# The state-space branch's state and output matmuls, each as four column tiles of 32

## The chip, the core and the metric

The kernel runs on one core of a Trainium2 chip. The metric is the device time of one execution, in microseconds (us). The engines are TensorE (PE; its weight loads are listed apart as PEld), VectorE (DVE), ScalarE (ACT), GpSimd (POOL) and SyncE (SP), which issues all transfers of this kernel. Each engine works through a queue of its own, in order, and waits at an instruction whose operands are not ready.

## What is computed

The program is a trunk of two layers on 256 tokens of width 1024. Each layer is a SwiGLU block, then four mixers side by side (RG-LRU, latent attention, sparse attention with an indexer, and S5), merged under gates, then a second SwiGLU block; every block is modulated by a vector that a product with `ada_w` gives. The change is in the S5 mixer. Cut to what matters here:

```python
def s5_branch(u, lam_re, lam_im, log_dt, b_re, b_im, c_re, c_im, d, w_glu, b_glu):
    # 32 groups of 16 channels, 64 complex states in each group
    ...
    ug = u.reshape(bsz, t, S5_GROUPS, S5_GROUP)
    bu_re = jnp.einsum('gpj,btgj->btgp', bb_re, ug)
    bu_im = jnp.einsum('gpj,btgj->btgp', bb_im, ug)
    _, _, x_re, x_im = lax.associative_scan(complex_combine, (a_re, a_im, bu_re, bu_im), axis=1)
    y = (jnp.einsum('gjp,btgp->btgj', c_re, x_re)
         - jnp.einsum('gjp,btgp->btgj', c_im, x_im))
    y = y.reshape(bsz, t, D_S5) + d * u
    y = jax.nn.gelu(y)
    return y * jax.nn.sigmoid(y @ w_glu + b_glu)
```

## The kernel before

**S5 by chunks.** The 256 tokens are 64 chunks of 4. Two groups of 16 channels make a pair, and there are 16 pairs `q`; one pair's 2 x 16 channels times 4 tokens of a chunk are the 128 partitions of `vv`, its 2 x 64 states the 128 rows of a state tile, and the 64 chunks are the moving columns. So every S5 matmul has 128 partitions, 128 stationary columns and 64 moving columns, in fp32. `s5_states` has four steps `h` in a layer; each puts 8 matmuls (2 parts z, real and imaginary, by 4 pairs) into one PSUM bank (L863), and DVE then turns, scans and turns back that bank and writes `F`, the state at the start of each chunk. `s5_out_prep` makes the stationary tiles for the outputs: `wo` (state to output) and `tz` (input of the chunk to its output); its own products, L817 and L820, are already written as four tiles of 32 columns (`tile_position=(0, 32 * qq)`), each tile with another moving operand. `s5_out` has two halves `h` of 8 pairs each; for each pair it adds up three products in PSUM, `tz` by `vv` (L898) and twice `wo` by `F` (L900). ACT and DVE make the GELU of each half.

**The precise products.** The large weights are fp32 and come by DMA into `raw` tiles. ACT rounds a tile to `hi` (the cast L237), DVE subtracts to get `lo` (through the helper at L103), and a product is three matmuls in the rounded type: `mm3` at L244 to L246, with weights moving, and `mm3w` at L249 to L251, with weights stationary. DVE operations go through helpers, so that L103, L106 and L109 are lines of helpers (tensor by tensor, scalar by tensor by tensor, tensor by scalar), L118 and L116 are copies on DVE and ACT, L112 is ACT's activation. `ada` (L277) also works in four tiles of 32 columns.

**What sets the order.** One string, `ORDER`, lists the stages of the mixers (S1 are the four steps of `s5_states`, S2 those of `s5_out_prep` and `s5_out`, m the steps of latent attention, g and p and t products for gates and merge). From the program in that order a scheduler sets each engine's queue. SBUF tiles are taken by tag from pools of a fixed number of buffers, and a tile waits until an earlier one of its tag is released: tag `s5p` has 7, and `tz`, `wo`, the merge's sums (`s5p_merge`) and the queries of latent attention (`s5p_mla`) all have it; `hi` and `lo` have 4 each, PSUM's `acc` has 4 and `up` 2.

**Latent attention beside it.** Around the outputs' run stands the first half of the heads: the product with `w_uq`, ACT's copy of it (L1306), the sums of squares (L1309), the scale `msc_mla` (L109, L1311), the rope of q (DVE, `s_rope` and `s5p_mla`), the transposes of q on PE (L1321), then the product with `w_ukv`, and the transposes of k (L1349). The matmuls of gate products (`ps_up_gate`) and of `tok_gemm` fill PE between them.

Of the kernel before, what the change touches and what calls it, by code (L numbers as in the profile page):

```python
# [78 lines left out]
def tile_trunk(ctx, tc, a, out, probe=None):  # L79
    nc = tc.nc  # L80
    V, S, T, G = nc.vector, nc.scalar, nc.tensor, nc.gpsimd
# [11 lines left out]
    def bank(tag, shape=(128, 512)):  # L93
        uid[0] += 1
        return ps.tile(list(shape), F32, tag="ps_" + tag, name=f"ps_{tag}_{lbl()}_{uid[0]}",
                       bufs=dict(acc=4, up=2, tp=1, ms=1)[tag])
# [17 lines left out]
    def cp(o, x, on_act):  # L114
        if on_act:
            S.copy(o, x)  # L116
        else:
            V.tensor_copy(o, x)  # L118
# [121 lines left out]
    def wpiece(w, k0, k, c0, n):  # L240
        return w[k0 * 128:(k0 + k) * 128, c0:c0 + n].rearrange("(k p) c -> p k c", p=128)
# [537 lines left out]
    def s5_out_prep(st):  # L779
# [49 lines left out]
        st["S2"] = (wo, tz)  # L829
        yield  # L830

    def w_stationary(w, c0, uh, ul, evac):

        for m in range(4):
            wt = W(8, 128, [(slice(0, 128), wpiece(w, 0, 8, c0 + 128 * m, 128))])
            p = bank("acc")
            for k in range(KD):
                mm3w(p[:, 0:256], wt.hi[:, k], wt.lo[:, k], uh[:, k], ul[:, k], k == 0, k == KD - 1)
            evac(m, p[:, 0:256])
# [6 lines left out]
    def s5_states(us, st):  # L846
        vv = new("b4", (128, 16, 64))
        v5 = vv.rearrange("p (b q) c -> p b q c", q=4)
        for i in range(4):
            for qq in range(4):  # L850
                o = v5[32 * i:32 * i + 32, :, qq, :]
                x = us[32 * qq:32 * qq + 32].rearrange("p b (c i) -> p b c i", i=4)[:, :, :, i]
                cp(o, x, KN["v"][qq])
        yield
        F = []
        st["S1"] = (vv, F)
        for h in range(4):
            qs = slice(4 * h, 4 * h + 4)
            p = bank("acc", (128, 2, 4, 64))
            for z in range(2):  # L860
                for q in range(4):
                    qg = 4 * h + q
                    T.matmul(p[:, z, q, :], st["wi"][z][qg // 8][:, qg % 8, :], vv[:, qg, :], start=True, stop=True)  # L863

            t = [new("p2", (128, 2, 4, 64)) for _ in range(2)]
            cs, sn = (bc(st[x][:, None, qs, :], (128, 2, 4, 64)) for x in ("cs", "sn"))
            tt(t[0], p, cs, OP.mult)
            tt(t[1], p, sn, OP.mult)
            tt(t[0][:, 0], t[0][:, 0], t[1][:, 1], OP.add)
            tt(t[0][:, 1], t[0][:, 1], t[1][:, 0], OP.subtract)  # L870
            fl = lambda x: x.rearrange("p q c -> p (q c)")
            mg = fl(st["mg"][:, qs])
            for z in range(2):
                V.tensor_tensor_scan(fl(t[1][:, z]), mg, fl(t[0][:, z]), 0.0, OP.mult, OP.add)

            if h % 2 == 0:
                zz = new("b4", (128, 2, 2, 4, 64))
            z = zz[:, h % 2]
            V.memset(z[:, :, :, 0:1], 0.0)
            d = slice(0, 63)  # L880
            tt(t[0], t[1], cs, OP.mult)
            tt(t[1], t[1], sn, OP.mult)
            tt(z[:, 0, :, 1:64], t[0][:, 0, :, d], t[1][:, 1, :, d], OP.subtract)
            tt(z[:, 1, :, 1:64], t[1][:, 0, :, d], t[0][:, 1, :, d], OP.add)
            F.append(z)
            yield

    def s5_out(l, st, r):
        yield from s5_out_prep(st)
        vv, F = st["S1"]  # L890
        wo, tz = st["S2"]
        y2 = new("b4", (128, 16, 64))
        for h in range(2):
            p = bank("acc", (128, 8, 64))
            for q in range(8):
                qg = 8 * h + q
                z = F[qg // 4]
                T.matmul(p[:, q, :], tz[h][:, q, :], vv[:, qg, :], start=True, stop=False)  # L898
                for zz in range(2):
                    T.matmul(p[:, q, :], wo[zz][h][:, q].rearrange("p i j -> p (i j)"), z[:, zz, qg % 4, :],  # L900
                             start=False, stop=(zz == 1))
            w = new("p2", (128, 8, 64))
            act(w, p, AF.Square)
            ts(w, w, 0.044715 * GK, GK, OP.mult, OP.add)
            tt(w, w, p, OP.mult)
            act(w, w, AF.Tanh)
            stt(y2[:, 8 * h:8 * h + 8], w, 1.0, p, OP.add, OP.mult)
            if h == 0:
                yield
        yc = new("b4", (128, 4, 256))  # L910
        y5 = y2.rearrange("p (b q) c -> p b q c", q=4)
        for i in range(4):
            for qq in range(4):
                o = yc[32 * qq:32 * qq + 32].rearrange("p b (c i) -> p b c i", i=4)[:, :, :, i]
                x = y5[32 * i:32 * i + 32, :, qq, :]
                cp(o, x, KN["y"][qq])
        show(f"s5y{l}", yc)
        r["yc"] = yc
        yield
# [675 lines left out]
    st = {}  # L1595
# [64 lines left out]
```

## Time and profile before

| | |
|---|---|
| time, median of 3 runs | 1500.77 us (1494.9 to 1513.13) |
| the profiled execution's own time | 1495.38 us |
| its span, first to last instruction | 1493.6 us |
| granted TensorE clock, mean of the span | 0.99 of full speed |
| PE / DVE / ACT busy | 1413.4 / 1175.4 / 770.0 us |
| DMA, mean over the span | 210 GB/s |

The profile is one execution; its times are counted from the span's start. Busy time is the union of an engine's instructions, including the time that a matmul is under way in the array, so neighbouring matmuls overlap and the distance from one start to the next says more than the length of one. Every fp32 matmul of the code has two records under PE (and two loads under PEld), every matmul in the rounded type has one. The two layers have the same code and the same order within the mixers; the first layer's S1 and S2 lie between 309 and 409 us, the second's from 1036 us on.

### The profile page before, as it was taken

How to read it: one execution, taken by the hardware profiler on the slowest of the kernel's cores; microseconds unless marked ns; L12 is line 12 of the kernel's file. 1: busy time of each engine (PE TensorE's matmuls, PEld its weight loads, DVE VectorE, ACT ScalarE, POOL GpSimd, SP SyncE). 2: the span in 40 equal slices, each digit the busy share in tenths (PEclk: the TensorE clock that was granted, in tenths of full speed). 3: DMA queues.
4: the chain of work that ended last, by engine and by line, in shares of the span. 5: the costliest groups of instructions: out<-in, count | busy, mean ns of one | idle time of the engine just before them, and what ended most of it. 6: DMA issues, size and time to landing. Idle time of an engine off the chain costs nothing.

```text
span 1493.6 us, 26644 instructions
## 1 busy us (share of the span) xinstructions
PE 1413.4 (95%) x10310; PEld 1262.7 (85%) x10310; DVE 1175.4 (79%) x2027; ACT 770.0 (52%) x1223; POOL 64.0 (4%) x75
## 2 busy tenths in 40 slices
PE   8899999899998998999989998999999999999998
PEld 4588987789888897999968887879988879799997
DVE  4598988789897577988787888777998956866655
ACT  4444456654475645544453445568445655544442
POOL 0000000001011000000010000000100100000000
PEclk9999999999999999999999999999999999999999
DMA  9788888786435365899977878755653535567762
GB/s 287 236 288 291 280 260 258 228 222 174 114 117 138 99 187 181 286 328 317 320 252 250 271 254 276 246 135 143 174 146 95 140 94 164 162 214 227 235 203 99
DMA packets 242087, 313.24 MB, mean 210 GB/s; under 512 B 28088, under 2 KB 169256, under 8 KB 241960
## 3 DMA queue, kind: packets, MB, share of 16 engines
q1 hardware_dynamic: 241960, 311.53, 67.0%
q8 instruction: 81, 1.33, 0.4%
q14 instruction: 46, 0.38, 0.1%
HBM read 310.41 MB, written 1.07 MB: 209 GB/s over the span
## 4 chain that ended last, share of the span: by engine, by line
PE 55%; DVE 21%; DMA 11%; issue 6%; ACT 5%; POOL 1%; SPq 1%; POOLq 0%; DVEq 0%; ACTq 0%
DVE lo_genexpr L103 7%; DMA raw_ada<-in_ada_w_dram 5%; PE ps_up_up_half L249 5%; PE ps_up_up_half L250 5%; PE ps_up_up_half L251 5%; DMA raw_init<-in_ffn_w_dram 4%; PE ps_acc_down_proj L246 3%; PE ps_acc_down_proj L245 3%; PE ps_acc_down_proj L244 3%; PE ps_up_gate L250 3%; ACT hi_genexpr L237 3%; PE ps_up_gate L249 3%; PE ps_up_gate L251 3%; DVE acc_ada L106 2%; PE ps_up_merge L250 2%
## 5 line engine op out<-in xcount | busy, mean ns | idle before, releaser
L237 ACT CAST hi_genexpr<-raw_init 128x1024 fp32r<-128x1024 f32 (+2 forms) x430 | 441.1, 1028 | 497.2 <-PE ps_up_up_half L250 127.4
L103 DVE TENSOR_TENSOR lo_genexpr<-raw_init,hi_genexpr 128x1024 fp32r<-128x1024 f32 (+2 forms) x430 | 511.5, 1193 | 152.5 <-ACT hi_genexpr L237 150.1
L249 PE MATMUL ps_up_up_half<-uh_new_u,hi_genexpr 128*128 128x256 f32 x1216 | 339.2, 279 | 4.2 <-DVE p_silu_cols L106 1.6
L250 PE MATMUL ps_up_up_half<-ul_new_u,hi_genexpr 128*128 128x256 f32 x1216 | 337.4, 278 | 0.0
L251 PE MATMUL ps_up_up_half<-uh_new_u,lo_genexpr 128*128 128x256 f32 x1216 | 337.2, 278 | 0.1
L249 PEld LDWEIGHTS ps_up_up_half<-uh_new_u,hi_genexpr 128*128 128x128 f32 x1216 | 228.8, 188 | 9.8 <-issue 7.5
L250 PEld LDWEIGHTS ps_up_up_half<-ul_new_u,hi_genexpr 128*128 128x128 f32 x1216 | 228.7, 188 | 1.4
L251 PEld LDWEIGHTS ps_up_up_half<-uh_new_u,lo_genexpr 128*128 128x128 f32 x1216 | 228.2, 188 | 0.7 <-DVE lo_genexpr L103 0.7
L106 DVE SCALAR_TENSOR_TENSOR acc_ada<-raw_ada,c_col_tile_trunk,acc_ada 128x1024 f32<-128x1024 f32 x105 | 134.4, 1280 | 28.6 <-DMA raw_ada<-in_ada_w_dram 28.2
L250 PE MATMUL ps_up_gate<-ul_new_u,hi_genexpr 128*128 128x256 f32 x512 | 144.8, 283 | 0.0
L249 PE MATMUL ps_up_gate<-uh_new_u,hi_genexpr 128*128 128x256 f32 x512 | 144.6, 282 | 0.0
L251 PE MATMUL ps_up_gate<-uh_new_u,lo_genexpr 128*128 128x256 f32 x512 | 143.6, 280 | 0.0
L246 PE MATMUL ps_acc_down_proj<-hi_genexpr,yT_mul_cols 128*128 128x512 f32 x288 | 114.6, 398 | 0.0
L244 PE MATMUL ps_acc_down_proj<-hi_genexpr,yT_mul_cols 128*128 128x512 f32 x288 | 114.5, 397 | 0.0
L245 PE MATMUL ps_acc_down_proj<-lo_genexpr,yT_mul_cols 128*128 128x512 f32 x288 | 114.3, 397 | 0.1
L249 PEld LDWEIGHTS ps_up_gate<-uh_new_u,hi_genexpr 128*128 128x128 f32 x512 | 96.4, 188 | 3.0 <-issue 2.2
L251 PEld LDWEIGHTS ps_up_gate<-uh_new_u,lo_genexpr 128*128 128x128 f32 x512 | 96.7, 189 | 0.9 <-issue 0.8
L250 PEld LDWEIGHTS ps_up_gate<-ul_new_u,hi_genexpr 128*128 128x128 f32 x512 | 96.4, 188 | 1.1 <-issue 1.0
L244 PEld LDWEIGHTS ps_acc_down_proj<-hi_genexpr,yT_mul_cols 128*128 128x128 f32 x288 | 54.1, 188 | 13.1 <-issue 1.6
L245 PEld LDWEIGHTS ps_acc_down_proj<-lo_genexpr,yT_mul_cols 128*128 128x128 f32 x288 | 54.2, 188 | 12.6 <-DVE lo_genexpr L103 0.6
L246 PEld LDWEIGHTS ps_acc_down_proj<-hi_genexpr,yT_mul_cols 128*128 128x128 f32 x288 | 54.1, 188 | 12.3
L244 PE MATMUL ps_up_tok_gemm<-hi_genexpr,uh_new_u 128*128 128x424 f32 (+2 forms) x88 | 33.8, 385 | 2.7 <-ACT gt_gate L112 2.7
(474 smaller groups left out, 2698.1 us busy)
## 6 DMA issues: line engine op xcount, KB each, us to landing
raw_init<-in_ffn_w_dram SPq DMA_DIRECT2D x240, 512.0 KB
raw_ada<-in_ada_w_dram SPq DMA_DIRECT2D x128, 512.0 KB
raw_init<-in_w_in_dram SPq DMA_DIRECT2D x96, 512.0 KB
raw_init<-in_w_branch_dram SPq DMA_DIRECT2D x24, 512.0 KB
raw_init<-in_ffn_w_dram SPq DMA_DIRECT2D x36, 256.0 KB
raw_init<-in_w_out_dram SPq DMA_DIRECT2D x16, 512.0 KB
s5p_load<-in_ada_w_dram SPq DMA_DIRECT2D x16, 256.0 KB
s5p_load<-in_ada_w_dram SPq DMA_DIRECT2D x8, 512.0 KB
```

The costliest lines, as they stand in the source:

```text
L103: eng.tensor_tensor(o, x, y, op)
L106: V.scalar_tensor_tensor(o, x, s, y, op0, op1)
L237: S.copy(self.hi, self.raw)
L244: T.matmul(o, xh, wh, start=first, stop=False)
L245: T.matmul(o, xh, wl, start=False, stop=False)
L246: T.matmul(o, xl, wh, start=False, stop=last)
L249: T.matmul(o, wh, xh, start=first, stop=False)
L250: T.matmul(o, wh, xl, start=False, stop=False)
L251: T.matmul(o, wl, xh, start=False, stop=last)
```

## The change

A helper `col_tiles` issues one old matmul as four: tile `j` has stationary columns 32j to 32j+31, the whole moving operand, and writes partitions 32j to 32j+31 of the same place in PSUM. The three calls of S5 (states, and both kinds of output products) go through it, and the four tiles follow one another by turns. All lines behind the helper move down by 6: L863, L898 and L900 become L836, L1321 becomes L1327. The 160 matmuls of both layers become 640.

```diff
@@ -829,6 +829,12 @@
         st["S2"] = (wo, tz)
         yield
 
+    def col_tiles(o, wt, x, start, stop):
+
+        for j in range(4):
+            c = slice(32 * j, 32 * j + 32)
+            T.matmul(o[c], wt[:, c], x, start=start, stop=stop, tile_position=(0, 32 * j))
+
     def w_stationary(w, c0, uh, ul, evac):
 
         for m in range(4):
@@ -860,7 +866,7 @@
             for z in range(2):
                 for q in range(4):
                     qg = 4 * h + q
-                    T.matmul(p[:, z, q, :], st["wi"][z][qg // 8][:, qg % 8, :], vv[:, qg, :], start=True, stop=True)
+                    col_tiles(p[:, z, q, :], st["wi"][z][qg // 8][:, qg % 8, :], vv[:, qg, :], True, True)
 
             t = [new("p2", (128, 2, 4, 64)) for _ in range(2)]
             cs, sn = (bc(st[x][:, None, qs, :], (128, 2, 4, 64)) for x in ("cs", "sn"))
@@ -895,10 +901,10 @@
             for q in range(8):
                 qg = 8 * h + q
                 z = F[qg // 4]
-                T.matmul(p[:, q, :], tz[h][:, q, :], vv[:, qg, :], start=True, stop=False)
+                col_tiles(p[:, q, :], tz[h][:, q, :], vv[:, qg, :], True, False)
                 for zz in range(2):
-                    T.matmul(p[:, q, :], wo[zz][h][:, q].rearrange("p i j -> p (i j)"), z[:, zz, qg % 4, :],
-                             start=False, stop=(zz == 1))
+                    col_tiles(p[:, q, :], wo[zz][h][:, q].rearrange("p i j -> p (i j)"), z[:, zz, qg % 4, :],
+                              False, zz == 1)
             w = new("p2", (128, 8, 64))
             act(w, p, AF.Square)
             ts(w, w, 0.044715 * GK, GK, OP.mult, OP.add)
```

On PE, at the first states step of the first layer, the order before is this (a name is tag, function, and two numbers; `ps_acc_s5_states` is the bank that the step fills, x4 says that four alike follow one another):

```order
L250 MATMUL ps_up_gate_623_3323<-ul_new_u_480_2577,hi_genexpr_629_3362 128x256
L251 MATMUL ps_up_gate_623_3323<-uh_new_u_479_2576,lo_genexpr_630_3363 128x256
L863 MATMUL ps_acc_s5_states_632_3397<-b4_s5_states_607_3211,s5p_s5_prep_280_1401 128x64 x4
L863 MATMUL ps_acc_s5_states_632_3397<-b4_s5_states_607_3211,s5p_s5_prep_282_1403 128x64 x4
L277 MATMUL ps_ms_ada_621_3291<-raw_ada_641_3428,c_col_tile_trunk_10_86 32x256 x4
L249 MATMUL ps_acc_w_stationary_642_3434<-uh_new_u_479_2576,hi_genexpr_639_3424 128x256
```

and now:

```order
L250 MATMUL ps_up_gate_623_3323<-ul_new_u_480_2577,hi_genexpr_629_3362 128x256
L251 MATMUL ps_up_gate_623_3323<-uh_new_u_479_2576,lo_genexpr_630_3363 128x256
L836 MATMUL ps_acc_s5_states_632_3397<-b4_s5_states_607_3211,s5p_s5_prep_280_1401 32x64 x16
L836 MATMUL ps_acc_s5_states_632_3397<-b4_s5_states_607_3211,s5p_s5_prep_282_1403 32x64 x16
L277 MATMUL ps_ms_ada_621_3291<-raw_ada_641_3452,c_col_tile_trunk_10_86 32x256 x4
L249 MATMUL ps_acc_w_stationary_642_3458<-uh_new_u_479_2576,hi_genexpr_639_3448 128x256
```

Each run of four matmuls of 128 columns has become sixteen of 32, in the same place, and what stands ahead and behind (a gate product, and ada's tiled one) is as it was.

On PE, at the first transposes of q of latent attention (L1321, now L1327), behind the outputs' run of the first layer and the product with `w_ukv`, before (`ps_up_gate_862` is the gate product between them, `hi_genexpr` and `lo_genexpr` its split weights, `s5p_mla_815` the queries):

```order
L250 MATMUL ps_up_gate_862_4749<-ul_new_u_480_2577,hi_genexpr_864_4752 128x256
L251 MATMUL ps_up_gate_862_4749<-uh_new_u_479_2576,lo_genexpr_865_4753 128x256
L249 MATMUL ps_up_gate_862_4749<-uh_new_u_479_2576,hi_genexpr_867_4782 128x256
...
L249 MATMUL ps_up_gate_862_4749<-uh_new_u_479_2576,hi_genexpr_867_4782 128x256
L1321 MATMUL ps_tp_mla_830_4576<-cst_tile_trunk_4_75,s5p_mla_815_4531 96x128 x4
L250 MATMUL ps_up_gate_862_4749<-ul_new_u_480_2577,hi_genexpr_867_4782 128x256
```

and now:

```order
L836 MATMUL ps_acc_s5_out_835_4788<-b4_s5_states_693_3819,s5p_s5_out_prep_730_4037 32x64 x4
L244 MATMUL ps_acc_mla_844_4917<-hi_genexpr_841_4912,mlh_mla_in_525_2756 128x512
...
L246 MATMUL ps_acc_mla_846_4926<-hi_genexpr_841_4912,mll_mla_in_526_2757 128x512
L249 MATMUL ps_up_gate_862_4989<-uh_new_u_479_2576,hi_genexpr_864_4992 128x256
L1327 MATMUL ps_tp_mla_830_4672<-cst_tile_trunk_4_75,s5p_mla_815_4627 96x128 x4
L250 MATMUL ps_up_gate_862_4989<-ul_new_u_480_2577,hi_genexpr_864_4992 128x256
L251 MATMUL ps_up_gate_862_4989<-uh_new_u_479_2576,lo_genexpr_865_4993 128x256
```

Ahead of the transposes stood 34 matmuls of the gate product, 24 with one weight tile and 10 with the next; now there is 1, and the other 33 are behind.

On DVE, at the rope of the same queries, before:

```order
L109 TENSOR_SCALAR msc_mla_817_4533<-mqs_mla_816_4532 128x8
L103 TENSOR_TENSOR lo_genexpr_875_4845<-raw_init_873_4842,hi_genexpr_874_4844 128x1024
L1311 TENSOR_SCALAR msc_mla_817_4533<-msc_mla_817_4533 128x8
L103 TENSOR_TENSOR s1_rope_825_4565<-s5p_mla_815_4531,tm_attn_prep_472_2541 128x128
...
L109 TENSOR_SCALAR p2_s5_out_834_4614<-p2_s5_out_834_4614 128x512
L103 TENSOR_TENSOR s5p_mla_815_4531<-s1_rope_825_4565,s1_rope_826_4566 128x8x16
L103 TENSOR_TENSOR s5p_mla_815_4531<-s1_rope_827_4567,s1_rope_828_4568 128x8x16
L103 TENSOR_TENSOR p2_s5_out_834_4614<-p2_s5_out_834_4614,ps_acc_s5_out_833_4589 128x512
L103 TENSOR_TENSOR lo_genexpr_880_4878<-raw_init_878_4875,hi_genexpr_879_4877 128x1024
L118 COPY s5p_mla_829_4575<-ps_tp_mla_830_4576 96x512
```

and now:

```order
L109 TENSOR_SCALAR msc_mla_817_4629<-mqs_mla_816_4628 128x8
L103 TENSOR_TENSOR s1_rope_825_4661<-s5p_mla_815_4627,tm_attn_prep_472_2541 128x128
L103 TENSOR_TENSOR s1_rope_826_4662<-s5p_mla_815_4627,tm_attn_prep_472_2541 128x128
L1317 TENSOR_SCALAR msc_mla_817_4629<-msc_mla_817_4629 128x8
...
L109 TENSOR_SCALAR p2_s5_out_834_4782<-p2_s5_out_834_4782 128x512
L103 TENSOR_TENSOR s5p_mla_815_4627<-s1_rope_825_4661,s1_rope_826_4662 128x8x16
L103 TENSOR_TENSOR s5p_mla_815_4627<-s1_rope_827_4663,s1_rope_828_4664 128x8x16
L103 TENSOR_TENSOR p2_s5_out_834_4782<-p2_s5_out_834_4782,ps_acc_s5_out_833_4685 128x512
L109 TENSOR_SCALAR p2_s5_out_836_4885<-p2_s5_out_836_4885 128x512
L118 COPY s5p_mla_829_4671<-ps_tp_mla_830_4672 96x512
L103 TENSOR_TENSOR lo_genexpr_875_5085<-raw_init_873_5082,hi_genexpr_874_5084 128x1024
```

The split `lo_genexpr_875` stood ahead of the rope (`s1_rope`) and now stands behind the copy of the transposed queries, 11 rows later; the rope's own rows keep their order. The same holds for the second layer. Further on, the transposes of k (L1349, now L1355) had 22 matmuls of `tok_gemm` between them and what stands ahead, and now have 5. The orders of SP and POOL are the same row for row.

## Rows read from the trace of the kernel before

**Rows 1.** The page's first part: busy us, share of span, instructions.

```profile
PE 1413.4 (95%) x10310; PEld 1262.7 (85%) x10310; DVE 1175.4 (79%) x2027; ACT 770.0 (52%) x1223; POOL 64.0 (4%) x75
```

**Rows 2.** The page's fourth part, the chain that ended last, by engine.

```profile
PE 55%; DVE 21%; DMA 11%; issue 6%; ACT 5%; POOL 1%; SPq 1%; POOLq 0%; DVEq 0%; ACTq 0%
```

**Rows 3.** Groups of instructions: tiles, shapes, count, busy us, mean ns, idle ahead.

```profile
L900 PE MATMUL ps_acc_s_out<-b_s_states,s5p_s_out_prep 128*128 128x64 f32 x128 | 19.5, 275 | 0.0
...
L863 PE MATMUL ps_acc_s_states<-b_s_states,s5p_s_prep 128*128 128x64 f32 x128 | 15.2, 272 | 0.9 <-DVE r_gate L106 0.9
...
L898 PE MATMUL ps_acc_s_out<-b_s_states,s5p_s_out_prep 128*128 128x64 f32 x64 | 12.3, 273 | 0.0
```

**Rows 4.** Timeline of PE, 394 to 412: start us, length us, instruction.

```profile
398.31 0.33 PE L898 MATMUL ps_acc_s_out<-b_s_states,s5p_s_out_prep 128*128 128x64 f32 x2
...
408.95 0.48 PE L244 MATMUL ps_acc_mla<-hi_genexpr,mlh_mla_in 128*128 128x512 f32 x1
...
410.41 0.28 PE L249 MATMUL ps_up_gate<-uh_new_u,hi_genexpr 128*128 128x256 f32 x1
410.53 0.28 PE L250 MATMUL ps_up_gate<-ul_new_u,hi_genexpr 128*128 128x256 f32 x1
```

**Rows 5.** Timeline of PE, 337.4 to 339.9, a states burst.

```profile
337.64 1.89 PE L863 MATMUL ps_acc_s_states<-b_s_states,s5p_s_prep 128*128 128x64 f32 x16
339.34 0.36 PE L249 MATMUL ps_up_gate<-uh_new_u,hi_genexpr 128*128 128x256 f32 x1
```

**Rows 6.** Timeline of PE, 380.3 to 383, tiled products of out_prep.

```profile
381.10 0.62 PE L817 MATMUL ps_acc_s_out_prep<-s5p_s_out_prep,s5bd_s_prep 128*32 128x128 f32 x16
381.54 0.24 PE L820 MATMUL ps_acc_s_out_prep<-p_s_out_prep,cst_tile_trunk 128*32 128x32 f32 x8
381.60 0.62 PE L817 MATMUL ps_acc_s_out_prep<-s5p_s_out_prep,s5bd_s_prep 128*32 128x128 f32 x16
```

**Rows 7.** Timeline of PE, 302.5 to 303.6, ada's product in a gate.

```profile
302.55 0.28 PE L251 MATMUL ps_up_gate<-uh_new_u,lo_genexpr 128*128 128x256 f32 x1
302.75 0.64 PE L277 MATMUL ps_ms_ada<-raw_ada,c_col_tile_trunk 128*32 128x256 f32 x8
303.55 0.28 PE L250 MATMUL ps_up_gate<-ul_new_u,hi_genexpr 128*128 128x256 f32 x1
```

**Rows 8.** Timeline of PE, 309.5 to 312.4, a states burst and ada.

```profile
309.68 1.89 PE L863 MATMUL ps_acc_s_states<-b_s_states,s5p_s_prep 128*128 128x64 f32 x16
311.50 0.64 PE L277 MATMUL ps_ms_ada<-raw_ada,c_col_tile_trunk 128*32 128x256 f32 x8
```

**Rows 9.** The page's third part, DMA queues: packets, MB, share of 16 engines.

```profile
q8 instruction: 81, 1.33, 0.4%
```

**Rows 10.** Windows: length, busy PE, PEld, DVE, ACT, POOL, clock, DMA, GB/s.

```profile
309.50:328.00 18.50, 18.50 (x171) 15.91 (x171) 16.14 (x36) 9.25 (x17) 1.27 (x2) 1.00 0.83 253
337.00:353.00 16.00, 16.00 (x142) 15.97 (x141) 15.30 (x35) 7.26 (x13) 1.39 (x2) 1.00 0.78 210
1036.00:1080.00 44.00, 43.13 (x339) 42.56 (x338) 43.65 (x94) 22.92 (x39) 3.62 (x4) 1.00 0.63 169
```

**Rows 11.** Timeline of DVE, 376 to 440; brackets: idle ahead, what ended it.

```profile
403.45 0.69 DVE L106 SCALAR_TENSOR_TENSOR s5p_merge<-gt_gate,ps_up_merge 128x512 f32<-128x512 f32 x1 [2.05 <-PE ps_acc_s_out L898]
...
409.08 0.17 DVE L109 TENSOR_SCALAR msc_mla<-mqs_mla 128x8 f32<-128x8 f32 x1
411.69 1.23 DVE L103 TENSOR_TENSOR lo_genexpr<-raw_init,hi_genexpr 128x1024 fp32r<-128x1024 f32 x1 [2.45 <-ACT hi_genexpr L237]
...
414.06 0.49 DVE L103 TENSOR_TENSOR s5p_mla<-s_rope,s_rope 128x128 f32<-128x128 f32 x2
```

**Rows 12.** Timeline of ACT, 376 to 440.

```profile
403.65 0.48 ACT L1306 COPY s5p_mla<-ps_acc_mla 128x384 f32<-128x384 f32 x1 [2.34 <-PE ps_acc_s_out L900]
```

**Rows 13.** Timeline of PE, 414 to 431.5, the transposes of q and k.

```profile
414.60 0.64 PE L1321 MATMUL ps_tp_mla<-cst_tile_trunk,s5p_mla 128*96 128x128 f32 x4
...
430.79 0.64 PE L1349 MATMUL ps_tp_mla<-cst_tile_trunk,s5p_mla 128*96 128x128 f32 x4 [1.07 <-DVE s5p_mla L103]
```

## The prediction

> **What bounds the kernel now.** I read the page's busy shares first: PE is busy for 95% of the span, DVE for 79% [rows 1]. The chain that ended last is more than half PE and a fifth DVE [rows 2], so PE time is worth something almost anywhere, unless DVE is as full where it is saved. The change touches three groups of matmuls: L863 (chunk states) and L898 and L900 (outputs), x128, x64 and x128 [rows 3]. Each fp32 matmul of the code makes two records, so these are 64, 32 and 64 matmuls, 160 in both layers. Their mean of 275 ns is a latency; what a matmul costs is the distance from start to start, read in the timeline. The output run of the first layer begins at 398.31 and the next matmul after it starts at 408.95: 96 records in 10.64 us, 0.111 each [rows 4]. A states burst of 16 records lasts from 337.64 to 339.34, 1.70 us [rows 5]. Beside it a 256-column record of the gate product takes only 0.12 (410.41 to 410.53) [rows 4], although it streams at least twice as much: a 64-column record is not paced by what it streams, but by what surrounds it, the load of 128 stationary columns.
>
> What column tiles cost can be read in this very kernel, since L817 and L820 already run as four tiles of 32 columns by turns, in fp32 [rows 6]. From 381.10 to 381.54 there are 16 records of 128 moving columns, from 381.54 to 381.60 eight of 32. Four tiles go side by side, so these are four groups of four at 0.11 and two groups at 0.03.
>
> **The change part by part.** *The burst itself.* An old matmul becomes four, of two records each: two groups of four. No row shows 64 moving columns in tiles. The nearest rows bound a group by 0.03 (32 columns) and 0.11 (128). I take the proportion, 0.03 + 0.08 x 32/96 = 0.057, because both rows are the same code shape, and the same pace for four loads is met at 0.03. Then a states burst takes 16 x 0.057 = 0.91 in place of 1.70 and saves 0.79; an output run takes 96 x 0.057 = 5.47 in place of 10.64 and saves 5.17. At 0.11 a group the saving would be nothing, at 0.03 it would be 1.22 and 7.8.
>
> *Going into tiles and out.* Ada's tiled product in the middle of a gate prices that: from L251 at 302.55 to L250 at 303.55 there is 1.00 us [rows 7]. Two ordinary matmuls are 0.23 of it, and two groups of 256 moving columns, by the same proportion, 0.22 each; 0.34 is left for the two changes. Two of the four states bursts of the first layer are directly followed by such an ada product [rows 8], which changes mode anyway, and the order keeps this. So six bursts and two output runs pay 0.34. PE saves 2 x 0.79 + 6 x 0.45 = 4.3 on states and 2 x 4.83 = 9.7 on outputs: 14.0 us.
>
> *Instruction stream.* 960 more matmuls are 3840 more PE instructions. PE's 20,620 records [rows 1] and 81 packets of 1.33 MB [rows 9] make 64 bytes each, 256 to a packet, so 15 more packets. An output run now draws three packets in 5.5 us, where the mean is one in 18. A packet took 0.4% x 16 x 1493.6 / 81 = 1.2 us [rows 9], so the bound is 0 to 3.6 us a run. I take 0: in the next step PE waits 3.1 us there anyway. [...]
>
> *What of the states' saving lands.* PE is covered without a gap in 309.5 to 328, and DVE has 2.4 us free there, of 18.5 [rows 10]; the first two bursts count in full, 1.6 us. In 337 to 353 DVE is at 15.30 of 16 [rows 10], and I count half of the next two, 0.45. In the second layer, over 1036 to 1080, DVE leaves 0.35 us of 44 free [rows 10]; PE would run up to DVE, so of four times 0.45 I count a third, 0.6. Sum 2.65.
>
> *What of the outputs' saving lands.* While PE does the first half of the run, DVE stands still for 2.05 us (until 403.45, ended by L898), and ACT's copy L1306 comes at 403.65, after 2.34 [rows 11, 12]. Both write tiles of the tag s5p, whose buffers the first half's stationaries hold. The half is 48 records; it now ends at about 398.31 + 48 x 0.057 + 0.2 = 401.2, so this wait goes. DVE's next one, 2.45 us before L103 at 411.69 (ACT, and behind it PE), goes too, since the new order puts that split behind the rope of q. What is late next is that rope. DVE needs 5.80 us from 403.45 to the end of L109 at 409.25, then 1.63 for the rope (from the end of the split at 412.92 to 414.55) [rows 11]. It is free from 401.4, so the rope is done at 408.8. PE ends the run at 398.31 + 5.47 + 0.34 = 404.1, the product with w_ukv 1.46 later [rows 4], one gate matmul at 405.7, and now meets the transpose of q, which the new order has behind 1 gate matmul in place of 34. It waits until 408.8: 3.1 us, and queued behind it are the gate's 33 other matmuls, whose operands are ready. Before, the transpose began at 414.60 with those 33 done [rows 13]. They still cost 33 x 0.117 = 3.9 us, so the gain is 414.60 - 408.8 - 3.9 = 1.9 us of 4.83. The second layer has the same code and order; I take 1.9 there too. Its ends are 0 (DVE gives it all back later) and 4.83 a layer. The next such place, the transpose of k at 430.79 that waited 1.07 for DVE [rows 13], now has 5 products of tok_gemm ahead of it in place of 22. PE waits longer there, with more left to do behind it while the softmax runs, and I put that at zero; if nothing covers it, 17 x 0.23 = 3.9 us a layer comes back.
>
> *Everything else.* Orders of SP and POOL are the same row for row, so no transfer moves in its queue. The clock was granted in full in these windows [rows 10]. Moving data are read four times as often, by tiles that L817 shows reading four different ones at once, at no extra price.
>
> **The sum.** 2.65 + 2 x 1.9 = 6.5 us. The profiled execution took 1495.38 us, 1493.6 of it span. The runs shown are 1494.9, 1500.77 and 1513.13, so it lies 5.4 below their median. I go from the mean of the two middle ones of these four, 1498.1, and predict 1491.6 us.
>
> **The rivals.**
> - *All of PE's saving lands*: 14.0 us, so 1484. For it speaks that PE is first in the chain [rows 2] and that DVE's waits in the run end on PE; against it that DVE is over 95% busy around six of the eight bursts.
> - *Records, not columns, set the pace.* L817 and L820 together are 24 records in 0.50 us (381.10 to 381.60), 0.021 each [rows 6]. If that is an issue rate, an old matmul is 8 x 0.021 = 0.167 us and saves 0.055. A burst gains 0.44 less 0.34, a run 2.6 less 0.34; PE saves some 6 us and about half lands: 1495. Against it: the eight records of L820 go by in 0.06, 0.0075 each. [...]
> - *The new order costs more than the burst saves.* PE waits 3.1 at the transpose of q and 3.9 at that of k, 7.0 against 4.83 saved, and nothing later takes it up: 2 x 2.2 lost, 2.65 won, 1500. It decides once DVE reaches the rope later than 410.5.
> - *Tiles run one after the other.* All four read the same moving address, which L817's do not. If each record then streams alone, an old matmul takes 8 x 0.057 = 0.45 us, 0.23 more; 160 of them on a full PE are 37 us: 1535, slower. It decides as soon as a group of four takes over 0.111. Against it stand the groups of L817, four at 0.11 together.
> - *The change doesn't do what it says*: the order has x16 and x4 of 32x64 where x4 and x1 of 128x64 stood, so this is left out.
>
> **How the numbers follow.** Forecast (gain of 4 to 11 us) 0.50; all of it 0.15; record pace 0.15; order 0.15; one after the other 0.05. The range must reach the first four: 1479 (1494.9 less 14 and some of the lower bound of a group) to 1504 (the order rival on a base of 1500.8, with a margin). Some 2% is about what a measurement of this kernel can tell from no change; only the last rival passes it upwards, and a gain over 30 us needs more than the 22 us that a group at 0.03 could give. Faster 0.02, same 0.92, slower 0.06.
>
> **What would show it.** Under the line of the new helper: a states burst of 64 records in about 0.9 us, an output run of 384 records in about 5.5, successive groups of four 0.057 apart. DVE's idle time before its first merge in the run under 0.5 us. PE waiting some 3 us, for DVE, at the transpose of q, at both layers. I am wrong if a burst isn't near half as long, if PE doesn't wait there, or if the time saved in the bursts reappears as waits in the attention that follows.

## The result, and the profile after

The changed kernel takes 1515.39 us (median of 19 runs, 1509.39 to 1525.01), the kernel before 1498.22 (median of 19, 1493.84 to 1513.13). The ratio is 1.0101, 95% interval 1.0081 to 1.0120: slower by some 15 us, where 1491.6 was forecast and 1479 to 1504 was the range. The profiled execution took 1516.49 us, 1514.7 of it span.

The page's first and third part after. PE is busy as long as before [rows 1], which hides a saving, as the first experiment shows; the instruction queue has 7 packets more [rows 9]:

```profile
PE 1412.9 (93%) x11270; PEld 1258.0 (83%) x11270; DVE 1179.6 (78%) x2027; ACT 770.7 (51%) x1223; POOL 63.3 (4%) x75
...
q8 instruction: 88, 1.44, 0.4%
```

The timeline of PE after, over a states burst that ada's product follows, one that a gate product follows, and the output run of the first layer:

```profile
307.85 0.28 PE L251 MATMUL ps_up_gate<-uh_new_u,lo_genexpr 128*128 128x256 f32 x1
308.06 1.10 PE L836 MATMUL ps_acc_s_states<-b_s_states,s5p_s_prep 128*32 128x64 f32 x64
308.98 0.61 PE L277 MATMUL ps_ms_ada<-raw_ada,c_col_tile_trunk 128*32 128x256 f32 x8
...
339.00 1.10 PE L836 MATMUL ps_acc_s_states<-b_s_states,s5p_s_prep 128*32 128x64 f32 x64
340.03 0.38 PE L249 MATMUL ps_up_gate<-uh_new_u,hi_genexpr 128*128 128x256 f32 x1
...
400.11 2.89 PE L836 MATMUL ps_acc_s_out<-b_s_states,s5p_s_out_prep 128*32 128x64 f32 x192
403.16 1.17 PE L836 MATMUL ps_acc_s_out<-b_s_states,s5p_s_out_prep 128*32 128x64 f32 x66 [0.17 <-ACT s5p_s_out_prep L116]
405.12 1.99 PE L836 MATMUL ps_acc_s_out<-b_s_states,s5p_s_out_prep 128*32 128x64 f32 x126 [0.80 <-issue]
407.04 0.50 PE L244 MATMUL ps_acc_mla<-hi_genexpr,mlh_mla_in 128*128 128x512 f32 x1
407.38 0.39 PE L245 MATMUL ps_acc_mla<-lo_genexpr,mlh_mla_in 128*128 128x512 f32 x1
408.58 0.39 PE L246 MATMUL ps_acc_mla<-hi_genexpr,mll_mla_in 128*128 128x512 f32 x1 [0.81 <-issue]
```

The tiles themselves do what was worked out: where ada follows, a burst of 64 records takes 0.92 us (308.06 to 308.98) in place of 1.82 [rows 8], where a gate product follows 1.03 (339.00 to 340.03) in place of 1.70 [rows 5], and the output run takes 6.93 (400.11 to 407.04) in place of 10.64 [rows 4], with two interruptions in it. (The longer one, 0.80, has "issue" in its bracket: PE waited for nothing that the profile shows.) So PE's saving is there, and the time is lost elsewhere. The timeline of PE further on, at the transposes of q, of k and of the second block's attention weights:

```profile
412.43 0.64 PE L1327 MATMUL ps_tp_mla<-cst_tile_trunk,s5p_mla 128*96 128x128 f32 x4 [2.65 <-DVE s5p_mla L103]
...
431.64 1.09 PE L1355 MATMUL ps_tp_mla<-cst_tile_trunk,s5p_mla 128*96 128x128 f32 x4 [3.97 <-DVE s5p_mla L103]
...
456.43 0.63 PE L1137 MATMUL ps_tp_attend<-cst_tile_trunk,p_attend 128*128 128x128 f32 x4 [2.58 <-DVE p_attend L103]
```

Before, the first of them began without a wait and the second after 1.07 us [rows 13]. Windows of 2 us just behind these waits (columns as in [rows 10]) show a second price: the granted clock, which falls to 0.50 of full speed (414 to 416 and 432 to 434):

```profile
412.00:414.00 2.00, 1.57 (x11) 1.58 (x12) 2.00 (x6) 1.00 (x3) 0.00 (x0) 0.83 0.01 4
414.00:416.00 2.00, 2.00 (x12) 1.88 (x11) 1.23 (x2) 1.27 (x5) 0.00 (x0) 0.50 0.00 0
...
428.00:430.00 2.00, 0.00 (x0) 0.00 (x0) 1.07 (x5) 1.37 (x2) 1.18 (x1) 1.00 0.18 51
430.00:432.00 2.00, 0.36 (x2) 0.35 (x3) 1.51 (x4) 1.12 (x2) 0.46 (x1) 0.59 0.60 211
432.00:434.00 2.00, 2.00 (x8) 1.69 (x7) 2.00 (x3) 0.68 (x1) 0.00 (x0) 0.50 0.03 8
```

And what DVE did meanwhile, in its timeline after, around the sums and scales of three norms (q, k, and the queries of sparse attention), with GpSimd's rows for the inverse roots in the second fence:

```profile
408.76 0.17 DVE L109 TENSOR_SCALAR msc_mla<-mqs_mla 128x8 f32<-128x8 f32 x1
408.83 0.49 DVE L103 TENSOR_TENSOR s_rope<-s5p_mla,tm_attn_prep 128x128 f32<-128x128 f32 x2
410.86 0.17 DVE L1317 TENSOR_SCALAR msc_mla<-msc_mla 128x8 f32<-128x8 f32 x1 [1.54 <-POOL msc_mla L326]
...
411.88 0.49 DVE L103 TENSOR_TENSOR s5p_mla<-s_rope,s_rope 128x128 f32<-128x128 f32 x2
...
430.49 0.49 DVE L103 TENSOR_TENSOR s5p_mla<-mkp_mla_in,mkr_mla 128x128 f32<-128x128 f32 x2 [1.36 <-POOL mkr_mla L326]
...
455.32 0.18 DVE L1242 TENSOR_SCALAR dsc_dsa<-dsc_dsa 128x16 f32<-128x16 f32 x1 [3.01 <-POOL dsc_dsa L326]
```

```profile
409.00 1.82 POOL L326 TENSOR_TENSOR msc_mla<-msc_mla,mhalf_tile_trunk 128x8 f32<-128x8 f32 x1 [23.52 <-DVE msc_mla L109]
428.82 1.64 POOL L326 TENSOR_TENSOR mkr_mla<-mkr_mla,mhalf_tile_trunk 128x8 f32<-128x8 f32 x1 [18.00 <-DVE mkr_mla L109]
452.38 2.90 POOL L326 TENSOR_TENSOR dsc_dsa<-dsc_dsa,mhalf_tile_trunk 128x16 f32<-128x16 f32 x1 [21.92 <-DVE dsc_dsa L109]
```

The helper `rstd` (L326) makes its sum on DVE, its power on GpSimd, and hands the result back to DVE. DVE works in order, so it stands for the whole trip, except for what lies between in its queue (at q, with two rows of the rope between, 1.54 us of GpSimd's 1.82). Before, a weight split lay there at q (the one at 411.69, [rows 11]); now it comes later. Over the whole program the waits for this line are, before, and after in the second fence (total us, times, longest):

```profile
DVE s5p_mla L103 <- POOL mkr_mla L326: 3.2, 2, 1.6
...
DVE msc_mla L1311 <- POOL msc_mla L326: 3.1, 2, 1.5
...
DVE dsc_dsa L1236 <- POOL dsc_dsa L326: 2.1, 2, 1.0
```

```profile
DVE msc_mla L1317 <- POOL msc_mla L326: 6.1, 4, 1.5
DVE dsc_dsa L1242 <- POOL dsc_dsa L326: 6.0, 2, 3.0
DVE s5p_mla L103 <- POOL mkr_mla L326: 5.9, 4, 1.6
```

8.4 us have become 18.0. To see where the time goes by stage I cut both traces at the same instructions: stretch A runs from the start of the 113th weight split on DVE (`lo_genexpr`, of 430) to the 131st, from just before the output run of the first layer to the end of its first half of attention; stretch B from the 319th to the 343rd is the same place of the second layer. The windows of A and B, before and after:

```profile
389.43:467.98 78.55, 73.59 (x531) 66.14 (x529) 70.11 (x188) 47.52 (x94) 8.22 (x4) 0.98 0.41 116
1096.75:1194.27 97.52, 90.08 (x765) 81.61 (x765) 88.19 (x222) 59.10 (x118) 8.20 (x4) 1.00 0.43 122
```

```profile
391.15:478.21 87.06, 74.42 (x818) 65.87 (x816) 71.30 (x188) 48.02 (x94) 8.16 (x4) 0.90 0.37 104
1108.85:1214.98 106.13, 91.39 (x1054) 81.85 (x1052) 89.32 (x222) 59.58 (x118) 8.09 (x4) 0.94 0.40 114
```

A is 8.5 us longer and B 8.6, together 17.1 of the 21.1 by which these two executions differ. DVE's busy time has grown by 1.2 and 1.1 us only; for the rest it stands. PE's clock is 0.90 and 0.94 in place of 0.98 and 1.00. (A and B are of one execution each. The part between them, 628.8 us before and 630.6 after, lies between 628 and 638 in the profiled executions of all runs, so differences of a few us from run to run prove little by themselves.)

### The profile page after: what moved, and what is told of

The parts are those of the page before. It is cut to its first block, busy times and chain, and to the rows that moved or that the text cites. A ratio compares the mean times of both kernels' runs of the same rounds, so it can differ in the third digit from the quotient of the medians.

```text
span 1514.7 us, 28570 instructions
## 1 busy us (share of the span) xinstructions
PE 1412.9 (93%) x11270; PEld 1258.0 (83%) x11270; DVE 1179.6 (78%) x2027; ACT 770.7 (51%) x1223; POOL 63.3 (4%) x75
## 3 DMA queue, kind: packets, MB, share of 16 engines
HBM read 310.41 MB, written 1.07 MB: 206 GB/s over the span
## 4 chain that ended last, share of the span: by engine, by line
PE 63%; DVE 20%; DMA 5%; ACT 5%; issue 5%; POOL 1%; SPq 0%; POOLq 0%; DVEq 0%; ACTq 0%
PE ps_up_up_half L249 7%; PE ps_up_up_half L250 7%; PE ps_up_up_half L251 7%; DVE lo_genexpr L103 6%; PE ps_acc_down_proj L246 4%; PE ps_acc_down_proj L245 4%; PE ps_acc_down_proj L244 4%; PE ps_up_gate L249 3%; PE ps_up_gate L250 3%; PE ps_up_gate L251 3%; DMA raw_ada<-in_ada_w_dram 3%; ACT hi_genexpr L237 2%; DMA raw_init<-in_ffn_w_dram 2%; PE ps_up_merge L250 2%; PE ps_up_merge L249 2%
## 5 line engine op out<-in xcount | busy, mean ns | idle before, releaser
L246 PEld LDWEIGHTS ps_acc_down_proj<-hi_genexpr,yT_mul_cols 128*128 128x128 f32 x288 | 54.1, 188 | 12.3
```

Source lines behind the costliest of these rows:

```text
L246: T.matmul(o, xl, wh, start=False, stop=last)
```

## The experiments

Two things had changed at once: the matmuls, and the order that the scheduler gave to everything around them. The first theory was "order", that the new order loses the time and the tiles gain; its rival "tiles", that tiles bring stalls for instructions, mode changes and a lower clock, whatever the order. They can be parted by holding the queues of PE, DVE, ACT and GpSimd to a given order (that of SyncE is the same in both kernels). All pinned kernels use this, with the list of positions taken from the program of before (old order) or from the changed one (new order); an S5 matmul counts as one position, however many tiles it has. The edges fix only the order of issue and add no wait. Each ratio below is to runs of the kernel before that were taken beside that run; their medians lie between 1498.4 and 1503.4 us, so ratios can be compared from run to run and times less well.

```diff
+def pin(tc, groups):
+...
+        line = [k for u in order for k in units[u]]
+        for x, y in zip(line, line[1:]):
+            tc.add_manual_dep(ins[y], x, dep, reason="pin")
```

**Tiles with the old order.** The matmuls of the change, every queue as before.

> All eight bursts and both output runs in four tiles, as in the changed kernel, but every engine's queue is held to the order that it had before the change. Theory 'order': the changed kernel's loss is the scheduler's new order (PE waits 2.7 us at the transposes of q and 4.0 at those of k in the first layer) and the half clock that is granted after those waits; with the old order these waits are about 1 us each as before, and the time is 1494 us (1486 to 1500), below the kernel before by some 4 us. [...]

Measured: 1493.47 us, ratio 0.9943 (0.9922 to 0.9964). The tiles gain 8.5 us where the order stays; if tiles lost the time whatever the order, this kernel would be as slow as the changed one. On its page PE is busy 13.9 us less than before, which is the 14.0 that was worked out for PE (the changed kernel has the same matmuls and is busy 1412.9; part of them run at the lower clock, 0.90 in A and 0.94 in B):

```profile
PE 1399.5 (94%) x11270; PEld 1244.4 (84%) x11270; DVE 1174.0 (79%) x2027; ACT 769.8 (52%) x1223; POOL 63.6 (4%) x75
```

The windows of A and B:

```profile
381.71:457.07 75.36, 67.90 (x819) 59.33 (x817) 69.94 (x188) 47.58 (x94) 8.22 (x4) 1.00 0.41 122
1091.32:1188.93 97.61, 87.26 (x1054) 77.82 (x1054) 88.21 (x223) 59.05 (x118) 8.21 (x4) 0.98 0.42 122
```

A is 3.2 us shorter than before, B as long as before; the waits for L326 are 8.5 us again. So the same tiles, held to the old order, beat both kernels.

**The old matmuls with the new order.**

```diff
-def col_tiles(o, wt, x, start, stop, n=4):
+def col_tiles(o, wt, x, start, stop, n=1):
```

> The matmuls of before (128 stationary columns, no tiles), but every engine's queue is held to the order of the changed kernel. Theory 'order': slower than before by 8 to 17 us, 1506 to 1515, since the transposes of k still stand too early and the half clock follows; the wait at the transposes of q should shrink, because PE gets there about 5 us later. Theory 'tiles': no difference from before, 1498 us within 3.

Measured: 1514.83, ratio 1.0106 (1.0053 to 1.0160). The order alone costs all that the change costs. "Tiles" is out: of the four combinations the two with the new order are at 1.010 and 1.011, the two with the old one at or below 1. It also shows that in the new order the tiles gain nothing that can be told (1.0101 with them, 1.0106 without).

**Parts of the tiles, old order.** States alone:

```diff
-                col_tiles(p[:, q, :], tz[h][:, q, :], vv[:, qg, :], True, False, 4)
+                col_tiles(p[:, q, :], tz[h][:, q, :], vv[:, qg, :], True, False, 1)
```

and the same for `wo`; then outputs alone, with 1 at the states.

> Only the states bursts in four tiles, output runs at 128 columns, old order on every engine. Each burst is 0.92 to 1.03 us in place of 1.70 to 1.87. Theory 'order': 1 to 3 us faster than before (1495 to 1497). Theory 'tiles': 0 to 4 us slower, most of the tiles' loss is in the outputs.

Measured: 1496.09, ratio 0.9970 (0.9943 to 0.9996): states alone gain, by an interval that just excludes no change.

> Only the output runs in four tiles, states bursts at 128 columns, old order on every engine. The run takes 5.4 us plus what PE stands in it for 'issue' (1 us in the first layer, 4.6 in the second, if the instructions come as late as in the changed kernel). Theory 'order': 0 to 4 us faster than before (1494 to 1498). Theory 'tiles': 6 to 12 us slower (1504 to 1510).

Measured: 1501.28, ratio 1.0006 (0.9983 to 1.0029). Outputs alone gain nothing. The profile's waits of PE give a part of the reason (engine line waited for: us, times, longest):

```profile
PE ps_acc_s_out L836 <- issue: 7.0, 4, 2.6
```

In its two runs PE stands 7.0 us (the changed kernel's runs had 0.80 and 3.9, not the 1 and 4.6 of the expectation) for nothing that the profile shows but its next instructions; the work of both shrinks by some 10 us together. Why the 3 us that are left don't show either is open. The parts add up to 0.24% and both together measured 0.57%; the intervals allow that, no more is to be read from it.

**Half the instructions.** Two tiles of 64 columns in place of four of 32 (n=2), old order.

> As the run with tiles and the old order, but two column tiles of 64 in place of four of 32: half as many instructions (an output run is 384 instructions, 1.5 blocks of 256, in place of 768). Theory 'supply': PE stands for 'issue' in the runs because instructions come no faster than a packet in 2 to 4 us; with half of them the standing falls from 2.8 and 3.5 us to under 1. If a group of two takes about as long as a group of four (0.06 us) the time is 1 to 4 us below that of the four tiles (1490 to 1492 where that was 1493.5); if it takes 0.09 to 0.11 the saving on PE is gone and the time is that of before, 1497 to 1500.

Measured: 1494.93, ratio 0.9958 (0.9933 to 0.9983), as with four tiles. In its timeline the second half of the run is 96 records in 2.95 us up to the next ordinary matmul, the change out of tiles included, so a group of two takes at most 0.061, about as long as a group of four:

```profile
393.41 3.02 PE L836 MATMUL ps_acc_s_out<-b_s_states,s5p_s_out_prep 128*64 128x64 f32 x96 [1.36 <-ACT s5p_s_out_prep L116]
396.36 0.50 PE L244 MATMUL ps_acc_mla<-hi_genexpr,mlh_mla_in 128*128 128x512 f32 x1
```

PE's waits for "issue" at the S5 lines are gone (with four tiles and the old order 3.0 us in the runs and 1.1 behind one), so they go with the number of instructions, as theory 'supply' has it. Its packet in 2 to 4 us is an estimate; the changed kernel's trace has 3 packets of the instruction queue from 399 to 411 us, around the first layer's run of 6.93. The 1 to 4 us that half the instructions were to bring don't show in the time; they are no more than the two intervals can tell apart.

**Where in the order.** All tiles, the same code with another list: the new positions over the states of both layers, the old ones elsewhere.

> All tiles; the new order only in the stretch of the states bursts of both layers, the old order from the output runs through the attention. Between the two traces the changed kernel fell behind by 3.4 us in the first layer's states and about 1 in the second's, by 10 and 9 us in the attention. Theory 'attention': 4 us slower than with the old order everywhere, 1497 to 1499. Theory 'both alike': half of the 22 us between the orders, 1503 to 1506.

Measured: 1498.30, ratio 0.9974 (0.9943 to 1.0004). Against 0.9943 with the old order and 1.0101 with the new, the states' part is 0.003, inside the uncertainty of some 0.004, and that of the runs and the attention 0.013.

**The clock.** PE kept busy where it waits, with matmuls into a bank that is overwritten next:

```diff
+    def awake(p, n, then):
+        g = [T.matmul(p, identb, maskb, start=True, stop=True).ins.name for _ in range(n)] + [then().ins.name]
```

> The changed kernel in its own order, but PE runs filler matmuls (bf16, 256 columns, into the bank that the transposes overwrite next) at the three places where it stood longest in each layer: 20 ahead of the first transposes of q, 30 ahead of those of k, 20 ahead of the first transposes of the attention weights. The waits stay, PE is only busy in them. Theory 'clock': most of the loss is the half clock granted behind the waits (412 to 417, 431 to 438 and 457 to 461 us in the first layer, some 7 us of PE time, as much in the second), so the granted clock stays 1.00 there and the time falls by 10 to 14 us, to 1501 to 1505 on a base of 1498. Theory 'waits alone': the time that PE stands is what counts, the fillers change nothing or cost a little: 1513 to 1518.

Measured: 1511.85, ratio 1.0073 (1.0044 to 1.0101), between the two theories. One set of fillers stood at the wrong transposes, so I moved it.

> As the run that kept PE awake in the new order, with the third set of fillers moved: there it stood ahead of the first block's transposes, where PE didn't wait, cost 2.2 us of PE and left the 2.6 us wait (and the half clock behind it) at the second block. Now 20 fillers ahead of the first transposes of q, 32 of k, 20 of the second block's attention weights. Theory 'clock and waits, about half each': over the stretch from the last states to the end of the first attention half the new order takes 11.7 us more than the old, of which 5.2 is standing and 6.5 is work stretched by a lower clock; the fillers give back 6 or so in each layer, so 1503 to 1506 on a base of 1500, a ratio of 1.001 to 1.005. Theory 'waits alone': as before the fillers were moved, less their 2.2 us twice, 1.005 to 1.007.

Measured: 1512.77, ratio 1.0102 (1.0076 to 1.0128). The ratio is above what both theories had. The windows of A and B:

```profile
389.17:470.62 81.45, 75.69 (x890) 66.52 (x888) 70.75 (x188) 48.13 (x94) 8.16 (x4) 1.00 0.40 112
1105.13:1208.16 103.03, 95.84 (x1129) 85.85 (x1127) 89.04 (x223) 59.81 (x118) 8.09 (x4) 0.98 0.42 118
```

The clock is 1.00 and 0.98 there, and they are 5.6 and 3.1 us shorter than in the changed kernel, of the 11.7 and 8.5 by which that one is longer than the tiles with the old order. That speaks for a third to a half of the loss in the stretches being work stretched by the lower clock, as expected there. But the whole time did not fall: in this execution the part between A and B is 3.9 us longer than in the changed kernel and the part behind B 1.9, and whether that is chance or comes of the fillers is not settled. Either way the loss is still there with the clock up, so the clock is not its first cause.

**Whose order.** All tiles; again only the list differs: PE's queue old, the others' new.

> All tiles; PE's queue in the old order, those of the other engines in the new one. Theory 'PE': what costs is that the transposes of q, of k and of the attention weights stand so early in PE's queue, ahead of matmuls that were ready; with PE's old order the loss is gone whatever DVE does: ratio 0.993 to 0.998. Theory 'DVE': what costs is that splits of weights moved behind the rope and PE then lacks weights: 1.004 to 1.010.

Measured: 1537.40, ratio 1.0260 (1.0236 to 1.0285), the slowest of all, A at 91.32 us and B at 113.28. Neither theory had that: putting the transposes back on PE alone doesn't give the loss back, it adds to it. PE's waits have moved (in A 6.2 us at the attention weights and 5.8 at `tok_gemm`). DVE's waits for L326 are 18.0 us in it, as in the changed kernel, so they don't explain the 24 us by which it is slower still, and those stay open. (PE's new order with DVE's old one was not run.) But waits that are the same in both slow kernels, and half as long in the kernel before and in the tiles with the old order, pointed to the trip to GpSimd.

**The trip to GpSimd taken out.** In both orders, a DVE operation of the same shape stands in place of the power. It writes 1.0, so these two kernels leave the inverse root out and serve for the time alone:

```diff
-        G.tensor_tensor(flat, flat, mhalf[:, 0:w], OP.pow)
+        g.append(V.tensor_scalar(flat, flat, 0.0, 1.0, OP.mult, OP.add).ins.name)
```

> All tiles and the new order, but the inverse root of the twelve norms of q, k and the scales in the mixers is not taken on GpSimd: a DVE operation of the same shape that writes 1.0 stands there, right behind the sum (q and k of the two attentions so stay without that factor). It takes a way from DVE to GpSimd and back (1.64, 1.82 and 2.90 us on GpSimd) out of DVE's queue. In the changed kernel's first layer DVE stands 7.5 us for it between the last states and the end of the first attention half, where the old order stands 2.6, because weight splits that stood between sum and root there now stand later. Theory 'trip': the new order costs as much as it does since these trips are no longer covered; without them PE's waits at the transposes of q and k shrink by 1.5 each and at the second block's weights by 2.6: 10 to 14 us less than the changed kernel, a ratio of 1.001 to 1.004. Theory 'queue of PE': the transposes stand too early whatever DVE waits for: 1.007 to 1.010.

Measured: 1495.53, ratio 0.9964 (0.9931 to 0.9997). That is some 20 us less than the changed kernel, where 10 to 14 were expected; the new order no longer costs anything against the kernel before. Its windows of A and B:

```profile
384.43:461.06 76.63, 68.78 (x807) 60.48 (x806) 71.41 (x192) 48.13 (x93) 0.00 (x0) 0.96 0.39 113
1096.18:1194.49 98.31, 89.30 (x1056) 80.13 (x1054) 89.82 (x227) 58.35 (x114) 0.00 (x0) 0.97 0.44 123
```

They are 10.4 and 7.8 us shorter than in the changed kernel, and within 1.3 of the tiles with the old order. PE's waits in A show where the trips had stood ahead of it, and where they had not:

```profile
PE ps_tp_mla L1356 <- DVE s5p_mla L103: 3.1, 1, 3.1
...
PE ps_tp_mla L1328 <- DVE s5p_mla L103: 0.4, 1, 0.4
PE ps_tp_attend L1138 <- ACT yT_s_glu L112: 0.3, 1, 0.3
```

At the transposes of q 2.65 us have become 0.4 and at the attention weights 2.58 have become 0.3, but at the transposes of k 3.1 of 3.97 stay (2.7 in the second layer).

> The same replacement (the inverse root left out, 1.0 in its place, on DVE) with all tiles and the old order. There DVE stands for GpSimd 2.6 us in the stretch, half of it beside other waits. Theory 'trip': a gain of 1 to 4 us against the tiles with the old order, a ratio of 0.991 to 0.994, so that of the 24 us between the orders 10 or so are the trips. Theory 'queue of PE': the same gain as in the new order, the difference between the orders stays at 0.013 to 0.016.

Measured: 1490.57, ratio 0.9933 (0.9902 to 0.9964), against 0.9943 with the trips. So without them the two orders lie 0.003 apart (0.9964 and 0.9933), and with them 0.016. Of the 24 us between the orders some 19 are these trips, with what follows from them (uncertain by some 8); the expectation had 10 or so. In DVE's own waits the difference is 9.5 us (18.0 against 8.5); the rest would be what these waits set off on PE, of which the windows show the lower clock.

## Why the prediction was wrong

**The burst**: right. A group of four records takes 0.056 (36 + 7 + 7 + 6 ns from start to start in the bursts), where 0.057 was taken between 0.03 and 0.11; a burst 0.92, where 0.91 was worked out. Tiles do not run one after the other (an old matmul takes two groups, 0.11, not 0.45), and records do not set the pace at 0.021 (64 in 0.92 are 0.014 each). That the load of 128 stationary columns sets the pace of the old matmuls stays the author's reading: before, PEld is busy for all of the 1.70 us of the burst at 337.64, but no run changed the load alone. PE's saving as a whole was right too (14.0 worked out, 13.9 measured with the old order), and had the order stayed, the forecast would have been met (0.9943, 8.5 us, where 6.5 was put). It reckoned with the new order, though, and that is where it failed.

**Into tiles and out**: 0.34 was too much. The first tile starts 0.21 after the last gate matmul (307.85 to 308.06), where ordinary ones are 0.12 apart, and the burst at 339.00 is 1.03 long to the next ordinary matmul, 0.11 more than the one that ada follows: 0.2 in all.

**Instruction stream**: the count was wrong, and zero was the wrong end of the bound for how long PE stands. 960 more matmul records bring as many loads, so 1920 instructions and 7 packets, not 3840 and 15 (20,620 records and 81 packets before, 22,540 and 88 after, so 255 and 256 to a packet). And PE did stand for them: 0.80 in the first layer's run and 0.81 right behind it, 3.9 in the second's, against a bound of 0 to 3.6 a run. The argument that PE would wait there anyway held all the same: in the first layer PE still stood 2.65 for the rope after that, and in the second it reached the transposes of q 0.2 after the rope was done (DVE's row ends at 1147.80), without a wait:

```profile
1143.60 2.23 PE L836 MATMUL ps_acc_s_out<-b_s_states,s5p_s_out_prep 128*32 128x64 f32 x75 [2.92 <-issue]
...
1148.01 0.60 PE L1327 MATMUL ps_tp_mla<-cst_tile_trunk,s5p_mla 128*96 128x128 f32 x4
```

So the wait at the transpose of q that was to show "at both layers" showed in the first alone. The two runs have the same 768 instructions for 5.4 us of work, and PE stood 0.80 us in one and 3.9 in the other. That such stops go when the instructions are halved speaks for PE waiting for its instructions; why one run waits so much longer than the other is not shown.

**What of the states' saving lands**: 2.65 us was put; with the old order 4.5 were measured (0.6 to 8.5), which doesn't contradict it.

**What of the outputs' saving lands**: the step that failed. "Rope done at 408.8" counts 5.80 us of DVE rows to the end of L109 and 1.63 for the rope. The first part was right: DVE comes to its first merge without a wait, and L109 ends 8.8 us after the run's start (400.11 to 408.93), where the prediction had 8.9 (398.31 to 407.2). The second left out that between L109 and L1317 lies the trip to GpSimd (1.82 on GpSimd alone). Before, DVE also stood there, but the row names ACT for it, since the weight split behind the sum was waiting for its cast; the trip ran beside that split's wait and work. I had read in the order that the split moves behind the rope, and took that as one wait less. It was the cover of another. The rope was done at 412.37 (411.88 and 0.49), 12.3 after the run's start where 10.5 was worked out, which leaves 0.1 of the 1.9 us of gain in that layer: the transposes come 12.3 after the run's start in place of 16.3, and the 33 matmuls behind them are 3.9. With the same trip at the other norms, which the prediction didn't look at, it comes to 19 of the 24 us between the orders.

**The transposes of k "at zero"**: not so. PE waited 3.97 there, where it had waited 1.07. A trip (1.36) lies ahead of it too, but the larger part is that PE comes to these transposes early, as the prediction had seen: without the trips 3.1 stay. With all trips out the new order costs 0.003 against the old one, some 5 us at both layers, so that is about what the zero was worth, with whatever else the order costs (uncertain by some 7). PE waited 2.6 more at the attention weights of the second block, behind the longest trip (3.01), at a place that the prediction did not look at.

**The rivals**: "the new order costs more than the burst saves" was the right one in kind, with 0.15. Its condition, DVE at the rope later than 410.5, was just met (12.3 after the run's start is 410.6 on the prediction's clock). Its price, 2 x 2.2 us, had neither the trips at the other norms nor the clock behind the waits (0.50 at 414 to 416 and 432 to 434), so its 1500 fell 15 short, and with it the range. The last of the signs of being wrong, time that reappears as waits in the attention that follows, is what came. What remains open is why the scheduler chose that order: its own estimates of durations were not looked into.

## What to carry to other kernels

Where a scheduler sets the order, a local gain is one experiment and the order that comes with it another: hold the queues to the old order, by edges that only fix the issue, and time the two apart. When an instruction moves away from between a producer and its consumer on an in-order engine, ask what round trip to another engine it was covering; a wait that the profile puts down to the last releaser can hide a second one that is almost as long. Column tiles paid here for fp32 matmuls with 64 moving columns, but in an output run, of 768 instructions, PE stood for them (0.80 us in one layer, 3.9 in the other): two tiles of 64 were as fast as four of 32 (ratios 0.9958 and 0.9943), with half as many instructions and without those stops.

## What was not expected of the hardware

A full-width fp32 matmul of 64 moving columns takes two records of 0.111; four tiles of 32 columns take two groups of 0.056, and two tiles of 64 two groups of at most 0.061, so half the width nearly halves the time and a quarter of it gives hardly more. Records of one group, which go to different tiles, start 6 to 7 ns apart, and the next group 36 ns behind the last of them. GpSimd's power on 128 x 8 elements takes 1.64 to 1.82 us, on 128 x 16 2.90.
